# The query scratch in DRAM in one piece, or in two by kind of row

## The chip, the cores and the metric

The kernel runs on one NeuronCore of a Trainium2 chip. The metric is the device time of one execution in microseconds; the median of three runs counts. All tensors are float32; a product is made of three TensorE passes over a split of each operand into a high part (`float32r`) and the rest.

## The reference

One layer of a hybrid encoder over two sequences (512 and 2048 tokens, 1024 features), each by itself. The attention group has 8 heads. A query or key of a head has 64 unrotated features and 32 that a rotary embedding has turned; the rotary key is shared by the heads.

```python
proj = rms_norm(x, norm1_g) @ w_in
c_q, c_kv, k_rope, u = jnp.split(proj, [256, 384, 416], axis=-1)
q  = (rms_norm(c_q, q_norm_g) @ w_uq).reshape(b, l, 8, 64 + 32)
kv = (rms_norm(c_kv, kv_norm_g) @ w_ukv).reshape(b, l, 8, 64 + 64)
q = concatenate([q[..., :64], apply_rope(q[..., 64:])])     # 96 features a head
k = concatenate([kv[..., :64], apply_rope(k_rope)])         # one rotary key for all heads
a = softmax(q @ k.T / sqrt(96)) @ v                         # per head, over the whole sequence
s = s5_bidirectional_glu(u, ...)                            # state-space group
x = x + concatenate([rms_norm(a), rms_norm(s)]) @ w_out
x = x + square(relu(rms_norm(x) @ w_mlp1)) @ w_mlp2         # then a last rms_norm
```

## The kernel before

The 2560 tokens are five blocks of 512 (`NB`), the first being the short sequence. Features lie on partitions, tokens on the free dimension. Two threads of Python generators emit instructions side by side at a pace of costs: `right` makes the projection `u`, then latents, queries, keys and values (`project_qkv`), then the attention; `left` makes the state-space group (`ssm`, 32 groups, reading `uT` and writing `gT`), the gate (`glu`), and the MLPs. Until the word "manual" (ahead of the first long attention job) a scheduler sets the order within each engine; after it the order is the one in which the code was written. Either way each engine then works through its own list in order, and so does SyncE, on whose queue all DMAs are issued (`dma`, L186).

Queries, keys and values go through DRAM, since the attention wants them in another arrangement. `qkv` (L434 on) makes, for one block, 14 PSUM tiles of 128 rows by 512 tokens in the order of the table `QKV`: 4 of keys, 4 of values, 2 of rotary query features (parts 4 and 5), 4 of unrotated ones (parts 0 to 3, each two heads of 64 rows). `put` empties one: ScalarE copies it to the high half of a tile `qk` (L189, for every second tile by way of a tile `ev`, L497), VectorE or GpSimd subtracts to make the low half (L192), and two steps later the tile, 128 rows of 2 x 512 values (512 KB), is written to DRAM. The pool of `qk` has two buffers (`QO`), so the copy into the third tile has to wait until the write of the first has landed.

The scratch for keys is `Ks[block, head, 64, 2, 512]`, for the rotary key `Kr[block, 32, 2, 512]`, for values `Vs`, for queries `Qs[block, head, 96, 2, 512]`, where rows 0 to 63 of a head are unrotated and 64 to 95 rotary. A part of the unrotated queries fills rows 0 to 63 of two heads (L537); a half of the rotary ones fills 16 rows of each of the eight heads (L552). In the attention a job has a tile `q` of 96 rows for two halves of 512 queries each, which `load_q` fills with one DMA. Its four short jobs (first sequence) are followed by 16 long ones (8 heads x 2 pairs of blocks); `load` issues K, Kr and then q for the job ahead, `maxpass` takes the row maxima (product L1055, VectorE L1057), and `tick` makes the scores (L1090 to L1092) and the sums with the values (L1114, L1116).

When `project_qkv` is through, its memory goes to the attention, whose first instructions there are VectorE's memsets of `onesel` (L1010).

Of the kernel before, what the change touches and what calls it, by code (L numbers as in the profile page):

```python
# [8 lines left out]
F32 = mybir.dt.float32  # L9
# [4 lines left out]
PSUM = bass.MemoryType.PSUM  # L14
# [4 lines left out]
NB = T // 512  # L19
# [69 lines left out]
def result(gen):  # L89
    """What a generator returns, its stages run at once"""  # L90
    while True:
        try:
            next(gen)
        except StopIteration as e:
            return e.value


def paced(state):
    """Generators side by side at the pace of the costs they yield; passes on what each adds"""
    while state:  # L100
        s = min(state, key=lambda s: s[:2])
        try:
            r = next(s[2])
        except StopIteration:
            state.remove(s)
            continue
        s[0] += r
        yield r


class Later:
    """Work to emit some steps after what it waits for"""
# [16 lines left out]
class Weights:  # L129
    """Weight tiles in the order of their use, loaded and split ahead of it"""  # L130
# [33 lines left out]
    def tick(self):  # L164
        """Before the use of tile clock, and half a tile into it"""
        c = self.clock
        if c % 1 == 0:
            self.rest(int(c) + self.LO)
        else:
            self.cast(int(c) + self.HI)  # L170
            self.load(int(c) + self.DMA)
        self.clock += 0.5
# [7 lines left out]
class Build:  # L180
# [38 lines left out]
    def columns(self, sq, dim, ps_pool, sp, ptag, keep=None, by=None):  # L219
        """(sum over features of sq / dim + eps) ** -0.5 of 128 tokens a column; a yield within.  # L220
        keep: a tile for it; by: columns that the features are still to be multiplied with"""
# [18 lines left out]
    def spread(self, c, ps_pool, ptag):  # L240
        """A PSUM tile with the columns of c as a row on every partition"""
        n = c.shape[-1]
        r = ps_pool.tile([128, 128 * n], F32, tag=ptag, name="rstd")
        for j in range(n):
            self.nc.tensor.matmul(r[:, 128 * j:128 * j + 128], c[:, j:j + 1].to_broadcast([128, 128]), self.ident,
                                  start=True, stop=True)
        return r

    def rstd(self, sq, dim, ps_pool, sp, ptag, keep=None, by=None):
        """The columns spread; stages by yields"""  # L250
# [5 lines left out]
    # ---------------------------------------------------------------- phase A  # L256
# [98 lines left out]
    def project_qkv(self, es):  # L355
        """Latents of a block alongside the queries, keys and values of the block before"""
# [77 lines left out]
    def qkv(self, b, c, normed, sp, op, pm, weights):  # L434
# [50 lines left out]
        def put(ps, shape, parts, view, store):  # L485
            """hi and lo of a PSUM tile: from it, or by way of SBUF"""
# [33 lines left out]
        # keys, values and the parts of the queries take turns  # L520
        for kind, m in QKV:
# [4 lines left out]
            elif kind == "v":  # L526
                tt = slice(m * 128, (m + 1) * 128)
                self.mm3(ps, ckh[:, tt], ckl[:, tt], kvh[:, 0, 512:], kvl[:, 0, 512:])
                # two heads side by side: [Vl Vh | Vh Vl]
# [3 lines left out]
            else:  # L533
                for k in range(2):
                    self.mm3(ps, uqh[:, k, cols(m)], uql[:, k, cols(m)], *cq[k], k == 0, k == 1)
                if m < 4:
                    put_rows(ps, lambda o, m=m: self.dma(self.Qs[b][2 * m:2 * m + 2, 0:64], o))  # L537
                else:
# [4 lines left out]
                    if m == 5:  # L543
# [4 lines left out]
                        def rope(r_, x):  # L548
# [3 lines left out]
                            later.add(4, lambda: self.dma(self.Qs[b][:, 64 + 16 * r_:80 + 16 * r_], o.bitcast(F32)))  # L552
# [7 lines left out]
    # ---------------------------------------------------------------- SSM  # L560
    def cmul(self, outr, outi, ar, ai, br, bi, t, engs, conj=False):
        """out = a * b, or a * conj(b)"""
# [9 lines left out]
    def ssm_prep(self, kp, tp):  # L572
# [44 lines left out]
        # unit phase and modulus of a^8  # L617
# [14 lines left out]
        # power tables  # L632
# [11 lines left out]
        # b_bar  # L644
# [18 lines left out]
        # [Re C, -Im C], one direction per column block  # L663
# [10 lines left out]
        # phase table: small powers 0..31, and the scalars E_32 .. E_256  # L674
# [27 lines left out]
    def ssm(self, es):  # L702
        """Groups follow each other at ten slots; every engine is given its work in the order of the slots"""
# [12 lines left out]
        def prep(gb):  # L716
            """(slot, stage)s of the matrices of a pair of groups, slots from the first of the pair before"""
# [29 lines left out]
            def kernel_rows():  # L747
                Mf = flat(t["M"])
                t["kw"] = kw = ps_y.tile([128, NG, 2, 16], F32, tag="y", name="kw")
                for g in range(NG):  # L750
# [3 lines left out]
                    # the zero lag is shared: the forward half of it and the skip  # L754
# [11 lines left out]
            def store():  # L766
                # row s of W holds lag 7 - s; output rows run backwards in time within a chunk
# [29 lines left out]
        def group(gg, t):  # L797
            """(slot, stage)s of a group, slots from its first product"""
# [41 lines left out]
            def rotate():  # L840
                # into the rotating frame; both planes are then real recurrences
# [22 lines left out]
            def unrotate():  # L864
                # the planes end up exchanged
# [53 lines left out]
    def glu(self, es, wp):  # L919
        """Gated SSM outputs, normalised and split"""  # L920
# [13 lines left out]
        def load(b):  # L934
            g[b] = gp.tile([128, 4, 512], F32, tag="g", name="g")
            gv = g[b].rearrange("p m (t j) -> p m t j", j=(64 if b == 0 else 256))
            # rows run backwards in time within a chunk
# [13 lines left out]
        def keep(b, m, t):  # L951
            """Twice an output, (tanh(z / 2) + 1) * g: split, and its part of the sum of squares"""
# [42 lines left out]
    # ---------------------------------------------------------------- attention  # L995
    def attention(self, es):
# [18 lines left out]
        # a job: two halves of 512 queries, each (head, query block, first of its 512-key slots, slots)  # L1015
# [3 lines left out]
        def load_q(job, pool=qp):  # L1019
            q = pool.tile([97, 2, 2, 512], F32R, tag="q", name="q")  # L1020
            (h, b, _, n), (h2, b2, _, _) = job
            src = self.Qs[b:b2 + 1, h] if n > 1 else self.Qs[b, h:h2 + 1:2]
            self.dma(q[0:96].bitcast(F32), src.rearrange("b p c j -> p b c j"))
# [6 lines left out]
        def load_v(e, v):  # L1030
            """v: (slots, key tiles, keys, [lo hi] or [hi lo])"""
# [50 lines left out]
        def tick(a=None, i=0):  # L1082
            """Scores of key tile i, split of the tile before it, values of the one before that"""
# [50 lines left out]
        def finish(a):  # L1134
            e = a.e
            PE.matmul(a.B, onesel[:, e], a.acc, start=False, stop=True)
            # e = 0: A = [Vl|Vh], B = [Vh|ones];  e = 1: A = [Vh|Vl], B = [ones|Vh]
# [19 lines left out]
        def run(job, q, plan, ahead=None):  # L1157
            """A job; plan: maxima to take on the way, each (generator, its length, first step, last step);
            ahead: (step, what loads the next job and plans its maxima)"""
# [33 lines left out]
        for j, job in enumerate(jobs):  # L1193
            plan, ahead = [], None
            if j < np_:
# [3 lines left out]
                if j == np_ - 2:  # L1199
                    # the first tiles of keys and values are free from here on  # L1200
# [21 lines left out]
    # ---------------------------------------------------------------- out-projection and MLP  # L1222
    def add_square(self, acc, x, k, late=None, scale=1.0):
        """late: the sum is VectorE's, and that of the tile before"""
# [11 lines left out]
    def pre_load(self, b, hx):  # L1236
        """The SSM half of the inputs of the out-projection"""
# [8 lines left out]
    def attention_half(self, b, h, l, pp):  # L1246
        """Attention outputs of block b over their row sums, normalised and split; l stages them"""
# [40 lines left out]
    def split(self, k, x, h, l, acc, scale=1.0):  # L1288
        """x times its gains, split, and its part of the sum of squares"""
# [15 lines left out]
    def ssm_half(self, b, h, l, pp):  # L1305
        """SSM outputs of block b, split; l stages them"""
# [6 lines left out]
    def mlp_pre(self, b, hx, pp, wo, loaded=None, tail=()):  # L1313
        """Attention and SSM outputs of block b -> residual stream and its normalised split.
        tail: what is left to do with the block before"""
# [83 lines left out]
    def mlp(self, b, side, last_in=None):  # L1399
        """side(): a generator to emit alongside, or None while there is none to start;  # L1400
        last_in: called when h and l are free"""
# [6 lines left out]
        def step():  # L1408
            """Every six products: what is due of the chains, of the weights and of the side"""
# [91 lines left out]
    def mlps(self):  # L1501
        self.streams = {}
        with ExitStack() as es, ExitStack() as es_r:
# [21 lines left out]
            def sides(b):  # L1525
                """The end of the block before and the start of the one after, alongside block b"""
# [35 lines left out]
    # ---------------------------------------------------------------- whole program  # L1562
    def scratch(self):
# [5 lines left out]
        self.Qs = d([NB, H, 96, 2, 512], F32, name="Qs")  # L1569
# [54 lines left out]
def drive(state, flags):  # L1624
    """Emit generators side by side at the pace of the costs they yield; a string waits for a flag.
    Returns the threads that none of the flags sets going any more."""
# [93 lines left out]
```

## Time and profile before

| | |
|---|---|
| median of 3 runs | 3834.84 us (3832.81 to 3836.03) |
| span of the profiled execution | 3829.5 us |
| TensorE busy | 3509.5 us (92%), 15248 products |
| VectorE busy | 2430.9 us (63%) |
| ScalarE busy | 1873.6 us (49%) |
| GpSimd busy | 1884.7 us (49%) |
| DMA | 400.24 MB, 105 GB/s in the mean |
| the chain that ended last | TensorE 63%, VectorE 15%, DMA 8%, issue 6%, GpSimd 4%, ScalarE 2% |

The span is one execution under the profiler, from its first instruction to its last; the run's time is 5.3 us longer in the median. Busy shares are means over stages that differ: the stage that matters here runs from some 255 us (first write of keys) to 729 us (start of the attention). The chain is followed back from the last instruction: at each step to what released it, or to the instruction before it on its engine. A piece that begins with DMA lasts from the issue of a transfer to its landing. A wait is the idle time of an engine just before an instruction, put down to what released that instruction last.

### The profile page before, as it was taken

The numbers are of one execution on the slowest core, as the hardware profiler recorded it, in microseconds if no ns is written. First come the engines' busy times: TensorE is split into PE (matmuls) and PEld (weight loads), VectorE is DVE, ScalarE is ACT, GpSimd is POOL, SyncE is SP. The second block draws the span as 40 slices with busy tenths as digits, with TensorE's granted clock in tenths as the row PEclk, the third lists the DMA queues.
The fourth block names the chain that finished last, engine by engine and source line by source line (L and its number), as shares of the span: only waits on it lengthen the run. The fifth ranks groups of instructions, "written<-read, shape, count | busy, mean of one in ns | idle before, by whom it ended". The sixth has DMA issues, their size and how long they took to land.

```text
span 3829.5 us, 46067 instructions
## 1 busy us (share of the span) xinstructions
PE 3509.5 (92%) x15248; PEld 2778.8 (73%) x15248; DVE 2430.9 (63%) x3540; ACT 1873.6 (49%) x3625; POOL 1884.7 (49%) x1552
## 2 busy tenths in 40 slices
PE   7877776398889999999999999999999999999998
PEld 6766664276667777777767677888888888888776
DVE  9588776567677676666676745545555555555545
ACT  5455454265566555556665663434333443434333
POOL 5467567135775555555577664423352335323321
PEclk9988787599999999999999999999999999999999
DMA  5333333464223333332332215223422252223322
GB/s 174 108 108 118 128 118 122 127 186 144 60 68 91 96 84 80 83 83 81 112 109 69 69 48 169 86 94 113 146 91 96 92 165 85 97 90 114 98 95 80
DMA packets 263761, 400.24 MB, mean 105 GB/s; under 512 B 51285, under 2 KB 120309, under 8 KB 263266
## 3 DMA queue, kind: packets, MB, share of 16 engines
q1 hardware_dynamic: 263522, 397.29, 34.4%
q8 instruction: 120, 1.97, 0.2%
q14 instruction: 119, 0.97, 0.1%
HBM read 325.52 MB, written 71.61 MB: 104 GB/s over the span
## 4 chain that ended last, share of the span: by engine, by line
PE 63%; DVE 15%; DMA 8%; issue 6%; POOL 4%; ACT 2%; SPq 1%; POOLq 0%; DVEq 0%; ACTq 0%
PE ps L198 14%; PE ps L196 14%; PE ps L197 14%; DMA Qs<-qk 3%; PE m L1055 3%; DVE wl L192 3%; PE s L1090 2%; PE s L1091 2%; PE s L1092 2%; PE B L1116 2%; PE A L1114 2%; DVE mx L1057 2%; DVE zl L192 1%; POOL acc L1231 1%; DVE pl L192 1%
## 5 line engine op out<-in xcount | busy, mean ns | idle before, releaser
L192 POOL TENSOR_TENSOR wl<-wr,wh 128x512 fp32r<-128x512 f32 x310 | 441.1, 1438 | 786.5 <-ACT wh L189 780.1
L1129 POOL TENSOR_TENSOR acc<-acc,ph 128x512 f32<-128x512 f32 x464 | 611.3, 1318 | 262.9 <-ACT ph L189 216.3
L196 PE MATMUL ps<-h,wh 128*128 128x512 f32 x1600 | 636.2, 398 | 1.4 <-DMA h<-sT 1.4
L1450 DVE TENSOR_TENSOR xa<-ps,xa 128x512 f32<-128x512 f32 x640 | 428.5, 685 | 323.5 <-PE ps L198 323.1
L198 PE MATMUL ps<-h,wl 128*128 128x512 f32 x1600 | 631.4, 395 | 1.1 <-POOL wl L192 1.0
L197 PE MATMUL ps<-l,wh 128*128 128x512 f32 x1600 | 630.9, 394 | 0.0
L189 ACT ACTIVATE wh<-wr 128x512 fp32r<-128x512 f32 x720 | 429.5, 621 | 315.3 <-PE ps L197 175.1
L1095 ACT ACTIVATE s<-s 128x512 f32<-128x512 f32 x544 | 316.8, 583 | 461.5 <-PE s L1092 423.2
L1057 DVE TENSOR_REDUCE mx<-m 128x1 f32<-128x512 f32 x544 | 371.5, 688 | 250.9 <-PE m L1055 244.7
L198 PE MATMUL ps<-zh,wl 128*128 128x512 f32 x1280 | 506.2, 395 | 8.0 <-DVE wl L192 3.9
L196 PE MATMUL ps<-zh,wh 128*128 128x512 f32 x1280 | 504.7, 394 | 1.1 <-ACT wh L189 1.0
L197 PE MATMUL ps<-zl,wh 128*128 128x512 f32 x1280 | 502.2, 392 | 0.0
L192 DVE TENSOR_TENSOR pl<-s,ph 128x512 fp32r<-128x512 f32 x544 | 369.0, 682 | 72.7 <-ACT ph L189 71.6
L192 DVE TENSOR_TENSOR wl<-wr,wh 128x512 fp32r<-128x512 f32 x410 | 385.5, 953 | 33.2 <-ACT wh L189 29.7
L192 DVE TENSOR_TENSOR zl<-t,zh 128x512 fp32r<-128x512 f32 x160 | 177.9, 1112 | 296.4 <-ACT zh L189 296.4
L196 PEld LDWEIGHTS ps<-h,wh 128*128 128x128 f32 x1600 | 302.3, 189 | 71.3 <-issue 3.4
L198 PEld LDWEIGHTS ps<-h,wl 128*128 128x128 f32 x1600 | 301.6, 189 | 72.1 <-POOL wl L192 2.8
L197 PEld LDWEIGHTS ps<-l,wh 128*128 128x128 f32 x1600 | 302.6, 189 | 70.0 <-issue 1.9
L189 ACT ACTIVATE ph<-s 128x512 fp32r<-128x512 f32 x544 | 325.3, 599 | 45.4 <-POOL acc L1127 1.4
L1432 ACT ACTIVATE t<-ps 128x512 f32<-128x512 f32 x160 | 95.6, 597 | 439.8 <-PE ps L198 435.8
L198 PEld LDWEIGHTS ps<-zh,wl 128*128 128x128 f32 x1280 | 240.7, 188 | 77.4 <-DVE wl L192 26.5
L1055 PE MATMUL m<-K,q 96*128 96x512 f32 x544 | 236.6, 439 | 59.0 <-DVE mx L1057 25.7
(308 smaller groups left out, 6442.2 us busy)
## 6 DMA issues: line engine op xcount, KB each, us to landing
wr<-w SPq DMA_DIRECT2D x640, 256.0 KB
wr<-w_out SPq DMA_DIRECT2D x80, 256.0 KB
K<-Ks SPq DMA_DIRECT2D x18, 1024.0 KB
V<-Vs SPq DMA_DIRECT2D x18, 1024.0 KB
q<-Qs SPq DMA_DIRECT2D x20, 768.0 KB
x<-xT SPq DMA_DIRECT2D x48, 256.0 KB
Ks<-qk SPq DMA_DIRECT2D x20, 512.0 KB
Vs<-qk SPq DMA_DIRECT2D x20, 512.0 KB
```

The source lines that it names most:

```text
L189: self.nc.scalar.activation(out, in_, AF.Copy, **kw)
L192: (eng or self.nc.vector).tensor_tensor(out, in_, hi.bitcast(F32), ALU.subtract)
L196: mm(ps, wh, xh, start=start, stop=False)
L197: mm(ps, wh, xl, start=False, stop=False)
L198: mm(ps, wl, xh, start=False, stop=stop)
L1055: PE.matmul(ps, q[0:96, i // 4, 0, i % 4 * 128:i % 4 * 128 + 128], Kt[h % 2][0:96, c0 + c, 0], start=True, stop=True)
L1057: V.tensor_reduce(mx[:, i, c:c + 1], ps, AX.X, ALU.max)
L1090: PE.matmul(ps, k[0:96, b, 1, ks], q[0:96, 0], start=True, stop=False)
L1095: S.activation(ps, ps, AF.Exp, scale=SCALE)
L1129: GP.tensor_tensor(o.acc, o.acc, h_.bitcast(F32), ALU.add)
L1432: S.activation(t, ps, AF.Relu)
L1450: V.tensor_tensor(xa[:, m0 + m], ps[m - m1], xa[:, m0 + m], ALU.add)
```

## The change

`Qs` becomes two tensors: `Qn[block, head, 64, 2, 512]` with the unrotated rows and `Qr[block, head, 32, 2, 512]` with the rotary ones. The write of a part of unrotated rows now fills two whole heads of `Qn`, which lie behind each other: one run of 128 rows. The write of a rotary half fills 16 of the 32 rows of each head of `Qr`. `load_q` fills the 96 rows of a tile `q` by two DMAs, 64 rows from `Qn` and 32 from `Qr`. Docstrings and comments are blanked besides; line numbers from 1023 on are one higher than before.

```diff
-                    put_rows(ps, lambda o, m=m: self.dma(self.Qs[b][2 * m:2 * m + 2, 0:64], o))
+                    put_rows(ps, lambda o, m=m: self.dma(self.Qn[b][2 * m:2 * m + 2], o))
...
-                            later.add(4, lambda: self.dma(self.Qs[b][:, 64 + 16 * r_:80 + 16 * r_], o.bitcast(F32)))
+                            later.add(4, lambda: self.dma(self.Qr[b][:, 16 * r_:16 * r_ + 16], o.bitcast(F32)))
...
             (h, b, _, n), (h2, b2, _, _) = job
-            src = self.Qs[b:b2 + 1, h] if n > 1 else self.Qs[b, h:h2 + 1:2]
-            self.dma(q[0:96].bitcast(F32), src.rearrange("b p c j -> p b c j"))
+            for part, rows in ((self.Qn, slice(0, 64)), (self.Qr, slice(64, 96))):
+                src = part[b:b2 + 1, h] if n > 1 else part[b, h:h2 + 1:2]
+                self.dma(q[rows].bitcast(F32), src.rearrange("b p c j -> p b c j"))
             return q
...
-        self.Qs = d([NB, H, 96, 2, 512], F32, name="Qs")
+        self.Qn = d([NB, H, 64, 2, 512], F32, name="Qn")
+        self.Qr = d([NB, H, 32, 2, 512], F32, name="Qr")
```

What the change makes of the engines' lists is seen at three places of SyncE's queue. In these rows a name is target<-source, and the sizes are those of the target as the DMA is issued; `T` and `U` are loads of the state-space group, `gT` and `Wd` its stores.

First, SyncE while the first block is made, at the first write of unrotated rows; before:

```order
L186 DMA T<-Wd_70 128x1x128 x2
L186 DMA U_606<-uT_58 128x1x64
L186 DMA U_606<-uT_58 128x1x256
L186 DMA Qs<-qk 2x64x1024
L186 DMA Qs<-qr 8x16x1024
L186 DMA gT<-ge 8x16x322
L186 DMA Ks<-qk 128x1024
L186 DMA Vs<-qk 128x1024
```

and now:

```order
L186 DMA T<-Wd_71 128x1x128 x2
L186 DMA U_607<-uT_58 128x1x64
L186 DMA U_607<-uT_58 128x1x256
L186 DMA Qn<-qk 128x1024
L186 DMA Qr<-qr 8x16x1024
L186 DMA gT<-ge 8x16x322
L186 DMA Ks<-qk 128x1024
L186 DMA Vs<-qk 128x1024
```

Nothing has moved; the write is 128 rows, as those of keys and values are, instead of 2 blocks of 64.

Second, SyncE at the end of that stage, where the last two writes of unrotated rows stand ahead of the attention's first loads; before:

```order
L186 DMA Ks<-qk 128x1024
L186 DMA Vs<-qk 128x1024
L186 DMA gT<-ge 8x16x322
L186 DMA Qs<-qk 2x64x1024 x2
L186 DMA U_607<-uT_60 128x1x64
L186 DMA U_607<-uT_60 128x1x256
L186 DMA K_6995<-Ks 64x4x1024
L186 DMA K_6995<-Kr 32x4x1024
```

and now:

```order
L186 DMA Ks<-qk 128x1024
L186 DMA Vs<-qk 128x1024
L186 DMA gT<-ge 8x16x322
L186 DMA Qn<-qk 128x1024 x2
L186 DMA U_608<-uT_60 128x1x64
L186 DMA U_608<-uT_60 128x1x256
L186 DMA K_6996<-Ks 64x4x1024
L186 DMA K_6996<-Kr 32x4x1024
```

Again the order is the same, and the writes alone differ.

Third, SyncE at the loads for one of the long attention jobs, between loads of MLP weights (`wr`) and the stores of the job before (`aT`, `sum`); before:

```order
L186 DMA q<-nm 1x4x128 x2
L186 DMA wr<-w 128x512 x2
L186 DMA K_6995<-Ks 64x4x1024
L186 DMA K_6995<-Kr 32x4x1024
L186 DMA q<-Qs 96x2x1024
L186 DMA wr<-w 128x512
L186 DMA aT_85<-al 64x512
```

and now:

```order
L186 DMA q<-nm 1x4x128 x2
L186 DMA wr<-w 128x512 x2
L186 DMA K_6996<-Ks 64x4x1024
L186 DMA K_6996<-Kr 32x4x1024
L186 DMA q<-Qn 64x2x1024
L186 DMA q<-Qr 32x2x1024
L186 DMA wr<-w 128x512
L186 DMA aT_86<-al 64x512
```

One transfer has become two, and what follows stands one place later in the queue; there are 20 such loads, and one store of `sT` has come between two loads of K elsewhere. The lists of TensorE and GpSimd are the same as before. On ScalarE two copies into `qk` stand one and three rows later at one place of the fourth block, among the tables of the state-space group, and on VectorE a subtraction into `qk` and a memset have changed places.

## Rows read from the trace of the kernel before

**Rows 1.** The chain that ended last, its shares of the span by line.

```profile
by line: PE ps L198 14.4%; PE ps L196 13.9%; PE ps L197 13.9%; issue 6.0%; DMA Qs<-qk 3.5%; PE m L1055 2.9%; DVE wl L192 2.7%; PE s L1090 2.5%; PE s L1091 2.4%; PE s L1092 2.4%; PE B L1116 2.3%; PE A L1114 2.3%; DVE mx L1057 1.6%; DVE zl L1
```

**Rows 2.** Stretches: length, busy PE, PEld, DVE, ACT, POOL (instructions), clock, DMA share, GB/s.

```profile
150.00:260.00 110.00, 87.59 (x529) 76.42 (x529) 96.58 (x147) 64.67 (x186) 61.95 (x75) 0.84 0.45 133
260.00:360.00 100.00, 67.95 (x367) 55.45 (x365) 79.35 (x105) 50.06 (x149) 64.44 (x73) 0.81 0.35 114
660.00:735.00 75.00, 24.80 (x81) 15.04 (x79) 32.30 (x45) 27.75 (x81) 26.67 (x35) 0.64 0.34 106
800.00:1000.00 200.00, 184.11 (x736) 137.57 (x735) 137.47 (x211) 112.76 (x199) 105.63 (x80) 0.96 0.50 145
```

**Rows 3.** The same chain in order of time, 271 to 729: start, us, what.

```profile
271.63 14.74 DMA Qs<-qk
...
319.05 10.16 DMA U<-uT
...
575.99 12.92 DMA Qs<-qk
...
686.37 10.58 DMA Wd<-ws
...
699.69 4.22 DMA Ks<-qk
...
707.93 20.89 DMA Qs<-qk
```

**Rows 4.** DMA issues by transfer: queue, operation, count, size of one.

```profile
Ks<-qk SPq DMA_DIRECT2D x20, 512.0 KB
...
Qs<-qk SPq DMA_DIRECT2D x20, 512.0 KB
```

**Rows 5.** Tile `qk`: what ended its engines' idle time (us in all, times).

```profile
  DMA Qs<-qk: 78.1, 12
  DMA Vs<-qk: 8.4, 2
  DMA Ks<-qk: 6.2, 5
```

**Rows 6.** Timeline at 286: start, us, instruction, [idle before <-releaser].

```profile
286.45 0.60 ACT L189 ACTIVATE qk<-mm 128x512 fp32r<-128x512 f32 x1 [8.12 <-DMA Qs<-qk]
...
287.08 0.69 DVE L192 TENSOR_TENSOR qk<-mm,qk 128x512 fp32r<-128x512 f32 x1 [6.29 <-ACT qk L189]
```

**Rows 7.** VectorE's waits, 255 to 735: us in all, times, longest.

```profile
DVE qk L192 <- ACT qk L189: 63.6, 12, 10.8
DVE r L845 <- POOL E L826: 24.0, 10, 7.9
...
DVE r L845 <- PE S L838: 8.6, 4, 3.3
```

**Rows 8.** VectorE's timeline, 690 to 731.

```profile
700.94 0.83 DVE L845 TENSOR_TENSOR r<-S,E 128x644 f32<-128x644 f32 x1 [7.89 <-POOL E L826]
...
728.99 0.11 DVE L1010 MEMSET onesel<- 128x64 f32 x1 [15.80 <-DMA Qs<-qk]
```

**Rows 9.** Two short stretches, columns as in rows 2.

```profile
714.00:727.00 13.00, 2.04 (x5) 0.58 (x3) 0.00 (x0) 5.44 (x18) 2.22 (x5) 0.53 0.16 62
700.00:704.00 4.00, 0.00 (x0) 0.00 (x0) 1.56 (x2) 1.52 (x7) 0.72 (x2) 0.50 0.80 288
```

**Rows 10.** Tiles `q` and `K`, issues: ns least/median/most, first and last start.

```profile
L186 SPq DMA_DIRECT2D q<-Qs x20: 349/430/1357, 593.7 to 2121.2; - x20
...
L186 SPq DMA_DIRECT2D K<-Kr x18: 584/594/1622, 729.6 to 2120.6; - x18
```

**Rows 11.** TensorE's waits, 700 to 2300: us in all, times, longest.

```profile
PE m L1055 <- DMA q<-Qs: 7.5, 3, 2.9
```

**Rows 12.** Sums of 16 stretches each: with a `Qs` write in flight, then without.

```profile
sum 268.00, PE 172.35 PEld 134.28 DVE 159.09 ACT 100.90 POOL 148.53; mean PE 10.77 PEld 8.39 DVE 9.94 ACT 6.31 POOL 9.28
...
sum 207.50, PE 148.66 PEld 119.06 DVE 173.04 ACT 126.37 POOL 144.77; mean PE 9.29 PEld 7.44 DVE 10.81 ACT 7.90 POOL 9.05
```

## The prediction

> **What bounds the kernel now.** I began with the chain of work that ended last. TensorE's products make up most of it; beside them stands a transfer: the 20 writes of unrotated query rows, `Qs<-qk`, hold 3.5% of the span [rows 1], 0.035 x 3829.5 = 134 us. The attention alone reads what it stores, so it should hold nothing of the stage ahead. Then I asked when. By stages [rows 2] TensorE is busy 92% of the time from 800 us on (184.11 of 200), but 68% at 260 to 360 and 33% at 660 to 735. VectorE goes the same way: 88% at 150 to 260, then 79% and 43%. ScalarE is at half, GpSimd at a third to two thirds. So the stage in which queries, keys and values are made beside the SSM has no engine at its limit; it waits.
>
> The chain within that stage [rows 3] names the wait. Nine of its pieces are a `Qs<-qk`, from 12.92 us to 20.89 in the last. Between them stands a write of a tile of the same shape and of the same 512 KB [rows 4], `Ks<-qk`, with 4.22 us. Two small transfers, a `U<-uT` and a `Wd<-ws`, take 10.16 and 10.58 us; both went out with a query write ahead of them.
>
> Who waits is in the view of tile `qk` [rows 5]: its pool has two buffers, so ScalarE's copy into one waits until the write before last has landed. That was `Qs` 12 times, 78.1 us in all, against 8.4 us for `Vs` and 6.2 us for `Ks`. ScalarE works in order, so all that stands behind that copy waits too. One instance [rows 6]: the copy starts at 286.45 after 8.12 us idle, and VectorE, which subtracts that copy, starts at 287.08 after 6.29 us idle. Over the stage [rows 7] VectorE waited 63.6 us in 12 waits for that copy. At its end [rows 8] the attention's first memset starts at 728.99 after 15.80 us: it needs memory from which the last `Qs` write still reads.
>
> Why is one write slow and the other not? Two stretches answer [rows 9]. From 714 to 727 the last two query writes are in flight, and two small loads issued behind them: the DMA engines are busy 0.16 of 16, about 2.6 engines, at 62 GB/s. From 700 to 704 a `Ks` and a `Vs` write are in flight: 0.80, about 13 engines, 288 GB/s. The query write goes out as 2 blocks of 64 rows, the key write as 128 rows. So I read the slow one as a transfer that about two engines carry, while a part of whatever follows queues on those two.
>
> [...]
>
> **The change part by part.** *Writes.* All 20 `Qs<-qk` of 2 x 64 rows become `Qn<-qk` of 128 rows, at the same places of SyncE's queue. Their target is one run of 512 KB, as that of `Ks`; I price the landing at that row's 4.22 us [rows 3]. The ten rotary writes keep their 8 x 16 rows and 4 KB runs: nothing.
>
> What this frees is counted on VectorE, the busiest engine of the stage, because a wait on ScalarE during which VectorE still works gains nothing:
> - End of the stage: the last write, issued at 707.93, would land at 712.2 and not at 728.8. VectorE had stopped at 713.2 (728.99 - 15.80), so all of the 15.8 us can go but for the start: 15.6.
> - The 12 waits for ScalarE's copy, 63.6 us. Behind them lie ScalarE's waits for `Qs`, `Vs` and `Ks`; the part of `Qs` is 78.1 / (78.1 + 8.4 + 6.2) = 84%, so 53.6. These end altogether if a write lands within 4.2 us: in the instance of [rows 6] the copy began to wait at 278.3 for a write issued at 271.63.
> - Transfers caught behind a query write: VectorE waited 24.0 us for GpSimd's `E` and 8.6 us for the product `S`, which itself waits for `U` [rows 7]. The longest of the first, 7.89 us until 700.94 [rows 8], ends just after the `Wd<-ws` of 10.58 us. I take half of that one and half of the 8.6: 8.
>
> Sum: 15.6 + 53.6 + 8 = 77. Late next is VectorE's own work, GpSimd's `E`, and `Vs` writes that go out behind a rotary one; these stay.
>
> *Reads.* Each of the 20 loads of 96 rows becomes one of 64 and one of 32, the same bytes in the same 4 KB runs. SyncE issues 20 more transfers, 0.43 us each [rows 10]. The load is the last of a burst (K, Kr, q). TensorE's maxima waited for it only 3 times, 7.5 us in all, the longest 2.9 [rows 11]. If the second half comes one issue later, that is 3 x 0.43 = 1.3 us; if its tail costs as much as the longest such wait each time, 3 x 2.9 = 8.7. I take 2, near the low end, since in the same burst `Kr` is itself a 32-row load that goes out one issue (0.594 us) after `K`'s 64 rows. A gain is excluded: no byte is saved. *Order.* TensorE's and GpSimd's instructions stand as they did; on ScalarE two `qk` copies stand one and three rows later among SSM work at one place, on VectorE one pair is exchanged. Nothing: a row there lasts some 0.6 us [rows 6], and there are fewer than ten such rows.
>
> [...]
>
> **Sum.** Net 77 - 2 = 75 us, all before 729. Past it the same work follows in the same order, so the span goes from 3829.5 to 3754.5. The median of the runs, 3834.84, lies 5.3 above the profiled span, which I carry along: 3760.
>
> **Bounds.** A second way of counting: the stage is parted [rows 12] into 16 stretches with a query write in flight (from its issue to the end of its piece of the chain, or 13 to 15 us where it is not on it) and the 16 ahead of and between them. In the first kind 268 us pass, with 159.09 of VectorE, 100.90 of ScalarE, 148.53 of GpSimd, 172.35 of TensorE; in the second 207.5 us, with 173.04, 126.37, 144.77 and 148.66. If the first kind ran at the busy share of the second, VectorE would need 159.09 / 0.834 = 191 us and save 77; ScalarE 166, saving 102; GpSimd 213, saving 55; TensorE 241, saving 27. The upper end by the chain: 134 - 9 x 4.2 = 96, and 6 each for `U` and `Wd`: 108.
>
> **Rivals.**
> 1. *Another engine is right behind* and becomes the bound: TensorE, at a granted clock of 0.64 to 0.84 of 2.4 GHz in this stage [rows 2], or GpSimd. For it: the 24.0 us that VectorE awaits GpSimd. Against: from 714 to 727 hardly anything runs. It saves 27 to 55: 3780 to 3808, middle 3794.
> 2. *The whole chain shortens*, since ScalarE runs ahead sooner and the transfers behind the writes land sooner. For it: 78.1 us on ScalarE alone. Against: VectorE worked through part of each wait. It saves 95 to 115: 3720 to 3740, middle 3730.
> 3. *The change doesn't do what it says*: the write is slow for something other than its two blocks. Then 128 rows take 13 us too, and the time is 3835. Against: `Ks`, 4.22 us.
> 4. *Slower*, by the split loads, in the 16 sample jobs of the attention, 800 to 2200 us. TensorE is the bound there, so each microsecond by which the 32-row half lands after its first use is lost. It decides from 75 / 16 = 4.7 us a job on; at twice the longest wait, 5.8 us, the time is 3835 - 77 + 93 = 3851. For it: the three waits of TensorE. Against: 17 of 20 loads had slack. [...]
>
> **Chances.** Forecast (saves 55 to 95: 3740 to 3780) 0.60; rival 1 0.18; rival 2 0.15; rival 3 0.04; rival 4 0.03. The range takes in rival 2 whole and rival 1 but for its last part: 3720 to 3802. About 0.2%, 8 us, is what a measurement tells from no change here: faster 0.93, within it 0.04, slower 0.03.
>
> **What would show it.** In the profile after, `Qn<-qk` is nearly gone from the chain, with pieces of 3 to 5 us; ScalarE's waits for it fall from 78.1 us to under 10, VectorE's for `qk` from 63.6 to about 10; the attention's first memset starts near 655, not 729; ahead of 260 and after the attention's start the stages keep their lengths. TensorE's waits for `q` stay under 10 us. If the write still takes 13 us, the reading of two engines is wrong; if it is fast and the stage hardly shorter, the step from waits to time is wrong, and the wait that VectorE then shows most of names what took over.

## The result, and the profile after

| | before | after |
|---|---|---|
| median | 3835.44 us (3832.81 to 3838.78, 4 runs) | 3749.66 us (3748.16 to 3752.27, 4 runs) |
| ratio, 95% interval | | 0.978 (0.9766 to 0.9794) |
| span of the profiled execution | 3829.5 us | 3746.4 us |
| attention's first memset starts | 728.99 us | 650.12 us |

The changed kernel is 85.8 us faster, in the range and inside the forecast's own 3740 to 3780. By the spans it gained 83.1 us, 78.9 of them before the attention starts. One execution among those below, of the kernel with two writes, took 4838.4 us in a slow state and is left out of its figures.

The page of the changed kernel: busy time of the engines, then the shares of the chain by engine.

```profile
PE 3495.4 (93%) x15248; PEld 2768.5 (74%) x15248; DVE 2439.0 (65%) x3540; ACT 1873.1 (50%) x3625; POOL 1892.0 (51%) x1552
...
PE 66%; DVE 16%; issue 6%; POOL 5%; DMA 4%; ACT 2%; SPq 1%; POOLq 0%; DVEq 0%; ACTq 0%
```

No engine has less to do; the busy times are those of before within about 0.4%. Transfers hold 4% of the chain where they held 8%.

The same stretches as in [rows 2], where these still exist (length, busy PE, PEld, DVE, ACT, POOL with instructions, clock, DMA share, GB/s):

```profile
150.00:260.00 110.00, 86.47 (x531) 74.66 (x530) 96.02 (x145) 64.60 (x186) 59.85 (x73) 0.86 0.44 127
260.00:360.00 100.00, 81.93 (x455) 66.06 (x453) 94.57 (x123) 53.90 (x160) 79.22 (x87) 0.88 0.46 145
```

Ahead of the first query write little changed. (The first write of keys goes out at 242.0 us in the kernel before, not at some 255; no wait for a copy lies between.) In the 100 us from 260 on VectorE is busy 94.57 us where it was 79.35: there an engine is near its limit. GpSimd went from 64.44 to 79.22, TensorE from 67.95 to 81.93, with a granted clock of 0.88 where it was 0.81 (means of its two levels, 0.50 and 1.00: products of 512 columns start 427 ns apart at the lower and 229 at the higher, medians in the kernel before).

The rest of the stage is not as full. All of it, from the first query write to the attention, of the kernel before and then of the changed one:

```profile
271.63:728.99 457.36, 305.90 (x1520) 240.86 (x1518) 315.93 (x433) 219.81 (x641) 279.82 (x322) 0.76 0.37 117
```

```profile
273.63:650.12 376.49, 289.71 (x1515) 232.13 (x1513) 323.71 (x433) 213.77 (x623) 284.52 (x316) 0.83 0.45 143
```

VectorE is busy 86% of the stage where it was 69%, TensorE 77% and GpSimd 76%.

The chain within the stage, in order of time (start, us, what); it answers to [rows 3]:

```profile
373.53 12.25 DMA Vs<-qk
...
446.11 7.69 DMA Qr<-qr
...
462.79 5.83 DMA U<-uT
...
617.13 4.59 DMA Qn<-qk
...
629.88 4.42 DMA Wd<-ws
...
637.07 3.81 DMA Ks<-qk
```

Nine pieces of 12.92 to 20.89 us have become one of 4.59. `U` and `Wd` are on it with 5.83 and 4.42 us where they took 10.16 and 10.58. The longest piece left is a write of values.

Tile `qk`, what ended ScalarE's idle time (us, times), as in [rows 5]:

```profile
  DMA Vs<-qk: 9.2, 2
  DMA Qn<-qk: 3.2, 3
  DMA Ks<-qk: 2.6, 3
```

VectorE's waits from 255 to 660 us, just past the attention's start (us in all, times, longest), as in [rows 7]:

```profile
DVE r L845 <- POOL E L826: 21.9, 9, 3.8
DVE c L473 <- PE rstd L245: 9.0, 5, 3.6
DVE qk L192 <- ACT qk L189: 6.3, 5, 2.0
...
DVE r L845 <- PE S L838: 4.1, 2, 2.1
```

And VectorE's timeline where the attention begins, as in [rows 8]:

```profile
649.33 0.83 DVE L870 TENSOR_TENSOR x<-Y,x 128x644 f32<-128x644 f32 x1
650.12 0.11 DVE L1010 MEMSET onesel<- 128x64 f32 x1
```

There is no bracket behind the memset: it starts as the instruction before it ends, and the 15.80 us of [rows 8] are gone. The wait for ScalarE's copy fell from 63.6 to 6.3 us; what VectorE now waits for most is GpSimd's `E`.

How long a write takes is worked out from the trace's semaphore events: from its issue to the last increment of its semaphore. In the stage `Qs<-qk` of before took 12.82 us at least and 13.79 in the median; `Qn<-qk` of after takes 2.59 and 3.89, and 7.25 at most. A stretch with one in flight, from 617.13 on, beside the end of a rotary write and two small loads, answers to [rows 9] (columns as above):

```profile
617.00:621.00 4.00, 3.21 (x11) 2.11 (x12) 3.32 (x5) 2.83 (x7) 4.00 (x4) 1.00 0.68 227
```

The DMA engines are busy 0.68 and move 227 GB/s, where the last two query writes of before had 0.16 and 62.

### The profile page after: what moved, and what is told of

It is laid out like the page before. It is cut to its first block, busy times and chain, and to the rows that moved or that the text cites. A ratio compares the mean times of both kernels' runs of the same rounds, so it can differ in the third digit from the quotient of the medians.

```text
span 3746.4 us, 46103 instructions
## 1 busy us (share of the span) xinstructions
PE 3495.4 (93%) x15248; PEld 2768.5 (74%) x15248; DVE 2439.0 (65%) x3540; ACT 1873.1 (50%) x3625; POOL 1892.0 (51%) x1552
## 4 chain that ended last, share of the span: by engine, by line
PE 66%; DVE 16%; issue 6%; POOL 5%; DMA 4%; ACT 2%; SPq 1%; POOLq 0%; DVEq 0%; ACTq 0%
PE ps L198 15%; PE ps L196 14%; PE ps L197 14%; PE m L1056 3%; DVE wl L192 3%; PE s L1091 2%; PE s L1092 2%; PE s L1093 2%; PE B L1117 2%; PE A L1115 2%; DVE mx L1058 2%; DVE zl L192 1%; PE mm L196 1%; PE mm L197 1%; PE mm L198 1%
## 5 line engine op out<-in xcount | busy, mean ns | idle before, releaser
L197 PEld LDWEIGHTS ps<-zl,wh 128*128 128x128 f32 x1280 | 241.6, 189 | 54.2 <-issue 1.0
```

The lines of the kernel that those rows point to most:

```text
L197: mm(ps, wh, xl, start=False, stop=False)
```

## The experiments

**Theories.** *Engines*: the write is slow since its outermost dimension, 2, lets two DMA engines carry it, as the prediction reads the DMA share of 0.16 in [rows 9]. *Layout* (rival): it is slow since its target lies in two runs, with the rotary rows between them; or the gain comes from the parting of the tensor or of the load. Then there is the question how a slow write costs time: *buffer*, the copy that waits for its tile, as [rows 5] have it, or *queue*, all that goes out behind it.

| kernel | median us | ratio to before, 95% | attention starts, us |
|---|---|---|---|
| two writes of 64 rows | 3754.37 | 0.979 (0.9775 to 0.9805) | 652.95 |
| padded heads | 3831.14 | 0.9991 (0.9982 to 1.0) | 724.6 |
| split load alone | 3833.68 | 0.9992 (0.9981 to 1.0002) | |
| four blocks | 3802.06 | 0.9918 (0.99 to 0.9936) | 700.3 |
| 18 idle writes, 2 blocks | 3843.2 | 1.0019 (1.0005 to 1.0032) | 737.7 |
| 18 idle writes, 128 rows | 3760.8 | 0.981 (0.9789 to 0.9832) | 654.5 |
| 2 idle writes at the end | 3775.61 | 0.9853 (0.9835 to 0.9872) | 668.0 |
| three buffers | 3848.3 | 1.0032 (1.002 to 1.0044) | 740.2 |
| its twin with two | 3834.15 | 0.9997 (0.9984 to 1.0009) | 744.1 |
| rotary 16 | 3745.06 | 0.976 (0.9747 to 0.9773) | 642.4 |
| rotary 16 again | 3744.1 | 0.9764 (0.9748 to 0.9779) | 644.5 |
| after again | 3750.34 | 0.9781 (0.9767 to 0.9795) | 646.55 |

**Two writes of 64 rows.** The kernel before, with `Qs` as it was and the load in one; only the write is issued once for each head.

```diff
-                    put_rows(ps, lambda o, m=m: self.dma(self.Qs[b][2 * m:2 * m + 2, 0:64], o))
+                    def each(o, m=m):
+                        for e in range(2):
+                            self.dma(self.Qs[b][2 * m + e, 0:64], o[64 * e:64 * e + 64])
+                    put_rows(ps, each)
```

> The kernel before, its scratch Qs and its single load of q untouched; only the write of unrotated rows is issued as two writes of 64 rows, one a head (40 instead of 20). Theory (the write is slow because its target is 2 blocks, which puts it on two DMA engines): each half lands in 3 to 4 us, the stage shortens as with the change, 3745 to 3757 us. Rival (the 96-row layout of the scratch, with its gaps, is what is slow): 3835 us. A few instructions of the last block stand in another order, worth some us either way.

It gains nearly what the change gains: 3754.37 us (3751.42 to 3759.29). The target is the same in the two runs as before, byte for byte. What each transfer's pattern has outermost is 64 rows, no longer 2 heads, and each of the 40 writes shows 16 increments of its semaphore where the 20 of before show 3. The wait of VectorE for the copy, 255 us to the attention's start:

```profile
DVE qk L192 <- ACT qk L189: 4.9, 3, 2.4
```

So the layout rival falls, and with it the notion that the tensor had to be parted.

**Padded heads.** The changed kernel, with one unused row behind the 64 of each head of `Qn`. The write is 2 blocks of 64 rows again; the instructions of the compute engines stand in the same order.

```diff
-                    put_rows(ps, lambda o, m=m: self.dma(self.Qn[b][2 * m:2 * m + 2], o))
+                    put_rows(ps, lambda o, m=m: self.dma(self.Qn[b][2 * m:2 * m + 2, 0:64], o))
...
+                src = src[:, 0:rows.stop - rows.start]
...
-        self.Qn = d([NB, H, 64, 2, 512], F32, name="Qn")
+        self.Qn = d([NB, H, 65, 2, 512], F32, name="Qn")
```

> The changed kernel with Qn padded to 65 rows a head, so that the write is 2 blocks of 64 rows again; two tensors and two loads of q stay, and the order on all compute engines is that of the changed kernel. Theory: the write lands in 13 to 15 us again and the whole gain is lost, 3832 to 3842 us, with ScalarE's waits for Qn back at 70 to 85 us. Rival (the gain comes from the tensors being apart, or from the loads): 3750 us.

The whole gain is lost: 3831.14 us, 0.9 under the forecast. Tile `qk` (what ended ScalarE's idle time), then VectorE's waits from 255 us to the attention's start:

```profile
  DMA Qn<-qk: 79.1, 12
```

```profile
DVE qk L192 <- ACT qk L189: 62.5, 13, 10.7
```

These are rows 5 and 7 of the kernel before almost to the number (78.1 and 63.6 us). The write lands 12.82 us after its issue at least. With the two runs together the cause is shown from both sides: with the old layout and 64 rows a transfer the time is gone, with the new tensor and 2 blocks it is back.

**Split load alone.** The kernel before, with the load of `q` in two.

```diff
-            self.dma(q[0:96].bitcast(F32), src.rearrange("b p c j -> p b c j"))
+            for rows in (slice(0, 64), slice(64, 96)):
+                self.dma(q[rows].bitcast(F32), src[:, rows].rearrange("b p c j -> p b c j"))
```

> The kernel before with the load of q alone split into 64 and 32 rows, from the one tensor Qs. Theory: plus 2 us, 3836 to 3839, TensorE's waits for q from 7.5 to about 10 us. Rival (the split costs in each of the 16 long jobs): plus 10 us or more.

The 2 us more that were forecast don't show: the ratio allows 7 us less to 1 us more. TensorE's maxima wait for the second load (600 to 2300 us):

```profile
PE m L1056 <- DMA q<-Qs: 9.8, 3, 3.5
```

against 7.5 us, also 3 times, in [rows 11]: 2.3 us, which the total does not show. Rival 4 falls.

**Four blocks.** The changed kernel with `Qn` in padded runs of 32 rows, two a head; a write is 4 blocks of 32, the load of `q` three transfers.

```diff
-                    put_rows(ps, lambda o, m=m: self.dma(self.Qn[b][2 * m:2 * m + 2], o))
+                    put_rows(ps, lambda o, m=m: self.dma(self.Qn[b][4 * m:4 * m + 4, 0:32], o))
...
-            for part, rows in ((self.Qn, slice(0, 64)), (self.Qr, slice(64, 96))):
+            halves = [self.Qn[:, r::2, 0:32] for r in range(2)]
+            for part, rows in zip(halves + [self.Qr], (slice(0, 32), slice(32, 64), slice(64, 96))):
...
-        self.Qn = d([NB, H, 64, 2, 512], F32, name="Qn")
+        self.Qn = d([NB, 2 * H, 33, 2, 512], F32, name="Qn")
```

> The changed kernel with Qn in padded runs of 32 rows, so that the write of unrotated rows is 4 blocks of 32 rows, and the load of q three transfers of 32 rows. Theory (as many engines as blocks): between 2 blocks (13.5 us median landing) and 16 engines (3.9 us), by the bytes an engine moves (256, 128, 32 KB) 3.9 + 96 x (13.5 - 3.9) / 224 = 8.0 us. Behind a wait that began some 7 us after the issue little is left then, so 15 to 35 us over the changed kernel: 3762 to 3785 us. Rival (any number of blocks over one is slow alike): 13 us and 3830 us; other rival (two blocks alone are slow): 4 us and 3752 us.

The direction is right and the size missed. The write takes 8.96 us at least and 10.76 in the median, and the kernel loses 52 us to the changed one, more than half of the gain. VectorE's waits from 255 us to the attention's start:

```profile
DVE qk L192 <- ACT qk L189: 30.4, 13, 4.2
DVE r L845 <- POOL E L826: 29.5, 13, 6.6
DVE onesel L1010 <- DMA bg<-b_glu: 10.0, 1, 10.0
```

The wait for the copy is half of that of before. The time of a write does not fall in proportion to its blocks: 12.82 us at least with 2, 8.96 with 4; the table further down has more.

**Idle writes.** The experiment on *how* a slow write costs time. The changed kernel gets 18 more writes, each issued right behind a `Qn` write, of 512 KB, from a weight tile that is not written again, to a scratch `Qx` that nobody reads. Nobody waits for a buffer of theirs. In one kernel they are 2 blocks of 64 rows (a head of `Qx` has 65), in its twin one run of 128 (64). All engines' lists stand in the same order in both.

```diff
+                        put = nc.sync.dma_start(out=self.Qn[b][2 * m:2 * m + 2], in_=o)
+                        if b < NB - 1 or m < 2:
+                            still = uqh.rearrange("p k c -> p (k c)")[:, 0:1024].bitcast(F32)
+                            with self.tc.issue_after(getattr(put, "ins", put)):
+                                self.dma(self.Qx[b][2 * m:2 * m + 2, 0:64], still)
...
+        self.Qx = d([NB, H, 65, 1024], F32, name="Qx")
```

> The changed kernel; behind each of the first 18 writes of Qn stands one more write of 512 KB from a weight tile that never changes, to a scratch that nobody reads, in 2 blocks of 64 rows. No buffer waits for it. Theory of the queue (what follows on the two engines waits for them to drain, so Ks, Vs and Qn writes behind it land late and their buffers with them): 30 to 65 us over its twin with 128 rows. Rival (the loss came from the buffer of the slow write alone): under 10 us over the twin.

> The twin of the kernel before in this list: the same 18 extra writes of 512 KB with the same order on every engine, but to one run of 128 rows. Theory: the bytes themselves cost little, 0 to 12 us over the changed kernel, 3750 to 3762 us. Rival (more traffic of any form delays the stage): as much as with 2 blocks.

3843.2 against 3760.8: 82 us between two kernels that move the same bytes with the same instructions, more than the 30 to 65 that were forecast. The slow transfer's own buffer is not in it. SyncE's queue, then the chain, of the kernel with 2 blocks:

```profile
301.03 0.39 SPq L538 DMA_DIRECT2D Qn<-qk  x1
301.48 0.54 SPq L186 DMA_DIRECT2D Qx<-w_uqh  x1
302.12 1.11 SPq L186 DMA_DIRECT2D Ks<-qk  x1
```

```profile
284.57 14.04 DMA Vs<-qk
...
302.12 14.58 DMA Ks<-qk
...
333.44 13.87 DMA U<-uT
```

A `Ks` write of 128 rows takes 14.58 us since it went out 0.64 us behind a `Qx`. Fourteen of the sixteen increments of its semaphore come early and two some 10 us later, here and in the kernel before (us after the issue).

| write of keys | goes out behind | 14th increment | 15th and 16th |
|---|---|---|---|
| at 302.12, 2 idle blocks | `Qx`, by 0.64 us | 4.08 | 14.57, 14.58 |
| at 298.47, before | `Qs`, by 0.64 us | 3.35 | 13.59, 13.79 |

In the second case the packet records of the trace have 16 packets of 4 KB in flight at 300.8 us, and two at a time from 301.5 to 311.7; the DMA share from 302 to 311 is 0.16. So I read the late part of the key write as one that stands behind the slow write on the two engines that carry it; the trace does not name the engines.

Of the 40 writes of keys and values the last two increments come over 3 us behind the other fourteen in 17 with 2 idle blocks and in 7 in the kernel before, all of them keys; in the twin and in the changed kernel it is none.

The waits of the kernel with 2 blocks, ScalarE's and then VectorE's (255 to 738 us):

```profile
ACT qk L189 <- DMA Ks<-qk: 92.5, 11, 9.6
```

```profile
DVE qk L192 <- ACT qk L189: 67.8, 12, 12.1
```

The twin's VectorE, 255 to 738 us:

```profile
DVE qk L192 <- ACT qk L189: 6.4, 3, 3.1
```

The views name `Ks` as the culprit, 92.5 us, and in nine of the eleven cases it is a victim, a write with two late increments. The bytes alone, with the other order that the scheduler makes of them, cost some 11 us (3760.8 against 3749.66 and 3750.34).

**Idle writes at the end alone.** The same, only behind the last two `Qn` writes.

```diff
-                        if b < NB - 1 or m < 2:
+                        if b == NB - 1 and m > 1:
```

> The changed kernel; only behind the last two writes of Qn stands an extra write of 2 blocks of 64 rows from the weight tile, which holds the memory that the attention's first memset needs. Theory (the end of the stage is a term of its own, 15.6 us): 10 to 18 us over the changed kernel, 3760 to 3768 us, with VectorE's wait of the memset 10 to 17 us. Rival (other loads would have kept the attention waiting anyway): under 5 us. SyncE has a load of q ahead of the K loads here.

The attention starts at 668.0 us, 17.9 later than in the changed kernel, and its first memset waits again:

```profile
DVE onesel L1016 <- DMA U<-uT: 16.2, 1, 16.2
```

The releaser is named `U<-uT`, but the memory there is that of the stage before, and a `Qx` write issued at 644.58 stands on the chain with 23.07 us. In the kernel before the same memset starts at 728.99, ahead of the last increment of either `U` load (729.05 and 729.74), so it does not wait for these. The end of the stage is thus a term of its own, 16.2 us by this wait, as the prediction had it. The total grew by 26 us, past the 10 to 18 that were forecast and 8 more than the start; in this kernel some loads after the start stand in another order, and what of the 8 that costs was not parted.

**Three buffers.** Were the buffer the point, a third one would free the copy. The kernel before with three buffers for `qk`; the room comes from `HB`, 10 to 9, and the twin has `HB` at 9 alone.

```diff
-HB = 10
+HB = 9
...
-                t["o"] = o = op.tile(shape, F32R, tag="qk", name="qk")
+                t["o"] = o = op.tile(shape, F32R, tag="qk", name="qk", bufs=3)
```

> The kernel before with three buffers of qk instead of two, and nine of xh and xl instead of ten, to make room. The write stays at 2 blocks. Theory of the queue (the transfers behind the slow write are late too, whoever holds the buffer): 10 to 40 us under its twin. Rival (the wait for the buffer was the loss): 60 to 80 us under its twin. The scheduler orders the two differently, worth some 10 us either way.

> The twin: the kernel before with nine buffers of xh and xl and two of qk, 3830 to 3850 us.

Both forecasts missed: the attention starts 4 us earlier than in the twin, and the time is 14 us worse. The start does not stand for the total in this pair; the twin starts the attention 15 us later than the kernel before at the same total. ScalarE's waits at tile `qk` with three buffers:

```profile
  DMA Qs<-qk: 53.5, 7
...
  DMA Ks<-qk: 19.4, 7
```

and with two:

```profile
  DMA Qs<-qk: 71.9, 10
  DMA Vs<-qk: 17.6, 5
  DMA Ks<-qk: 17.6, 9
```

A third buffer takes a third of ScalarE's wait away, but VectorE's wait for the copy is 58.1 us against 59.6, and the last write holds the attention's memory all the same (14.6 and 15.0 us). The scheduler also orders the work another way with it, so the 14 us are not parted into their causes. What is shown is that a buffer more, in this order, does not buy the gain.

**Rotary 16.** What is late next is the write of rotary rows (8 blocks of 16). It is treated in the same way: the rows of a head are stored so that a half of them is 16 blocks of 8 rows, and the rotary keys in the same order, in two writes.

```diff
-        later.add(4, lambda: self.dma(self.Kr[b], ko.bitcast(F32)))
+        def store_kr():
+            for r_ in range(2):
+                self.dma(self.Kr[b].rearrange("(a r e) c j -> a r e c j", a=2, r=2)[:, r_],
+                         ko[16 * r_:16 * r_ + 16].bitcast(F32))
+        later.add(4, store_kr)
...
-                            later.add(4, lambda: self.dma(self.Qr[b][:, 16 * r_:16 * r_ + 16], o.bitcast(F32)))
+                            later.add(4, lambda: self.dma(self.Qr[b].rearrange("h (a r e) c j -> (h a) r e c j", a=2, r=2)[:, r_], o.bitcast(F32)))
```

> The changed kernel with the rotary rows of a head stored in the order (half of 8, part, row), so that the rotary write is 16 blocks of 8 rows instead of 8 blocks of 16; Kr is stored in the same order by two writes of 16 rows instead of one of 32. Compute engines keep the order. Theory (engines are set by the number of blocks): the rotary write lands in 3.5 to 5 us instead of 6 to 7.5, the Vs writes behind it sooner, 5 to 15 us less than the changed kernel, 3735 to 3745 us. Rival (eight engines are as good as 16, or the new bound is the compute): 3748 to 3752 us.

> The kernel with 16 rotary blocks once more, on the same chip as the changed kernel. Theory (rotary writes on 16 engines free the Vs writes behind them; the attention started 7.7 us earlier in its trace): 3 to 9 us under the changed kernel. Rival (compute is the bound by now): within 2 us of it.

> The changed kernel once more, beside the one with 16 rotary blocks: 3745 to 3755 us.

The rotary write lands in 4.25 us in the median where it took 7.63, and the `Vs` write behind it, 12.25 us in the changed kernel, is on the chain with half:

```profile
371.02 6.07 DMA Vs<-qk
```

ScalarE's wait for `Vs` at tile `qk` falls from 9.2 to 0.4 us. Both times its median is the lowest of all, 3745.06 and 3744.1 us, 4.6 and 6.2 below the changed kernel, at the edge of the first forecast and within the second. But the intervals of the ratios overlap, so this gain is likely and not shown.

## Why the prediction was right

| step | predicted, us | measured, us |
|---|---|---|
| landing of the write | 4.22 | 2.59, 3.89, 7.25 (least, median, most) |
| end of the stage | 15.6 | 15.80, no wait left |
| waits for the copy | 53.6 of 63.6 | 57.3 (63.6 to 6.3) |
| behind the writes: `E` and `S` | 8 | 6.6 (24.0 to 21.9, 8.6 to 4.1) |
| reads: TensorE's wait for `q` | 2 | 2.3 (7.5 to 9.8) |

**The write** went as read: 2 blocks are slow, 128 rows are not, and rival 3 falls with the landing of `Qn` and with the padded heads.

**The sum.** The three gains make 79.7 us against 77. From the first query write to the attention the stage shrank from 457.4 us (728.99 - 271.63) to 376.5 (650.12 - 273.63), by 80.9. The step that was mis-sized is the share of the copy's wait that ends: by ScalarE's waits I kept 16% for `Vs` and `Ks`, 10 us, and 6.3 are left. `Vs` and `Ks` do hold ScalarE as before (11.8 us in all against 14.6), as predicted; VectorE has work meanwhile. The two halves in the 8 us were guesses that came near: the waits for `E` fell by 2.1 us and not 3.9.

That 79.7 and 80.9 are so close is in part luck, as two things that the sum left out cancel. VectorE's other waits shrank too: its idle time in the stage went from 141.4 us to 52.8, by 88.6, some 9 more than the three terms. And its same 433 instructions took 7.8 us longer (315.93 to 323.71). The rest of the 83.1 comes after the attention's start, 4.2 us. That is within what two executions of the changed kernel differ by: the other profiled one has a span of 3737.8 us and starts the attention at 646.55.

**Rival 1**, an engine right behind, didn't come: over the stage VectorE stayed the busiest, with 323.71 us against 289.71 of TensorE and 284.52 of GpSimd. The count by stretches had 27 to 55 us for these two because it held them to their busy shares of 72% and 70% in the other stretches; they went to 77% and 76%. VectorE's 77 us in that count is the forecast again. That VectorE sets the pace now is read from its share; no run made one of the engines faster. (The clock of 0.84 that this rival names is that of the stretch ahead of the stage; within it [rows 2] have 0.81 and 0.64. The 2.4 GHz beside it stand in no row. They agree with the lower level, where 512 columns in 427 ns are 1.2 a ns, if a column is a cycle; at the higher one 229 ns make 2.24.) **Rival 2** asked for 95 us or more.

**Rival 4** didn't come: the split load alone measured 0.9992 (0.9981 to 1.0002). Two transfers for one gained nothing at the load, and most of the gain at the write, where two halves in place of one transfer with 3 increments measured 0.979. The loads have slack here; nothing is shown on kernels where they have none.

**Where the reading was too narrow.** The prediction tells of two costs, the copy that waits for its buffer and transfers caught behind, and books 53.6 us to the first and 8 to the second. The idle writes show that a loss as large needs no slow buffer: with slow transfers whose buffers nobody needs, 82 us are lost, and then it is `Ks` that the copy waits for. All of it lies ahead of a memset that doesn't wait, while the query writes of before cost some 65 us there (80.9 less the 15.8 at the end); that both totals come near 82 is a coincidence.

In the kernel before both are at work. Seven of its key writes were late behind a query write and landed 1.2 to 4.7 us after it. No copy waited for these seven, since the wait for the query write's buffer covered theirs; that they would have been next, had that buffer been free, is argued and not shown. But the buffer costs by itself, too. The query write issued at 375.96 has no other write from `qk` behind it until it lands at 388.78, and ScalarE's copy and VectorE wait for it all the same:

```profile
388.88 0.60 ACT L189 ACTIVATE qk<-mm 128x512 fp32r<-128x512 f32 x1 [5.37 <-DMA Qs<-qk]
...
389.51 0.69 DVE L192 TENSOR_TENSOR qk<-mm,qk 128x512 fp32r<-128x512 f32 x1 [5.14 <-ACT qk L189]
```

How the 83 us part into the two stays open. The sum came out near since it was counted on the waiting engine, not on the releaser's name.

## What to carry to other kernels

Look at the outermost dimension of both sides of every DMA: a pattern with 2 there, where the rows could be one run or two transfers, can delay what is issued behind it on the same queue while it is in flight (a `Ks` write took 14.58 us here, and 4.22 in [rows 3]), and the views may then put the time down to whichever transfer was waited for. On the chain such a transfer shows as a write with no reader near, several times as long as one of the same size (here 12.92 to 20.89 us against 4.22). If the layout can't change, issue one transfer a block: here two writes of 64 rows gained nearly as much as the new layout (0.979 against 0.978). A load that has to be split for the new layout costs little where the loads have slack (0.9992 for the split alone).

## What the runs showed of the hardware

Time from issue to the last increment, all of 512 KB, in this stage:

| pattern | transfer (kernel) | least us | median us | increments seen |
|---|---|---|---|---|
| 2 x 64 rows | `Qs` (before) | 12.82 | 13.79 | 3 |
| 2 x 64 rows | `Qn` (padded heads) | 12.82 | 13.56 | 3 |
| 4 x 32 rows | `Qn` (four blocks) | 8.96 | 10.76 | 5 |
| 8 x 16 rows | `Qr` (after) | 5.98 | 7.63 | 9 |
| 16 x 8 rows | `Qr` (rotary 16) | 3.71 | 4.25 | 16 |
| 128 rows | `Qn` (after) | 2.59 | 3.89 | 16 |

By the least times, twice the blocks take 0.6 to 0.7 of the time, not half: from 2 to 4 blocks 12.82 became 8.96, and here the expectation for four blocks went wrong. Nor does the number of increments alone set it: 16 blocks of 8 rows and 128 rows both show 16 increments, and take 3.71 and 2.59 us. The increments seen are one more than the blocks with 2, 4 and 8 of them, and 16 with 16 blocks and with 128 rows; why one more is not shown. They go with what the DMA engines do where a write has them nearly to itself, by the packet records and the DMA share:

| write (kernel) | stretch, us | packets of 4 KB in flight, median | DMA share of 16 engines | increments |
|---|---|---|---|---|
| `Qs`, 2 x 64 rows, at 375.96 (before) | 378 to 388 | 2 | 0.16 | 3 |
| `Qr`, 8 x 16 rows, at 527.63 (after) | 529.2 to 532.4 | 8 | 0.49 | 9 |
| `Qn`, 128 rows, at 398.65 (after) | 399.7 to 400.4 | 16 | 1.01 | 16 |

In the first stretch four small `Wd` stores are in flight as well. So the prediction's reading of two engines agrees with these records.

A second thing concerns the issue on SyncE. The load of 96 rows in one took 0.430 us to issue [rows 10]; its two halves take 0.640 and 0.630, each more than the whole. Tile `q`, issues (ns least/median/most, first and last start):

```profile
L186 SPq DMA_DIRECT2D q<-Qn x20: 583/640/902, 551.3 to 2038.4; - x20
...
L186 SPq DMA_DIRECT2D q<-Qr x20: 579/630/1267, 552.0 to 2039.1; - x20
```

The prediction had 0.43 us more a load; it is 0.84, and the three waits of TensorE for `q` grew by 2.3 us in all. The write got cheaper instead, 0.352 us (tile `qk`) where the 2 x 64 rows of the padded kernel take 0.550:

```profile
L186 SPq DMA_DIRECT2D Qn<-qk x20: 319/352/647, 273.6 to 644.9; - x20
```

```profile
L186 SPq DMA_DIRECT2D Qn<-qk x20: 511/550/590, 272.0 to 703.7; - x20
```

Why the load of 96 rows issues in less than its halves stays open.
